# Weights of a hybrid decoder layer handed over as contiguous tiles, gate columns as one array, trial layouts of the fifth FFN pair removed

## The chip, the cores and the metric

The kernel runs on one core of a Trainium2 chip; the other cores are idle. The metric is device time in microseconds (us) of one launch. TensorE (PE) multiplies, with the loads of its stationary operand shown apart as PEld; VectorE (DVE) and ScalarE (ACT) do the elementwise work; GpSimd (POOL) does a few small operations; SyncE (SP) issues nearly all DMAs, which sixteen DMA engines carry out between HBM (DRAM) and the on-chip buffer.

## The reference

One layer of a decoder over 512 tokens of width 2048, in float32. With `h = RMSNorm(x)`, one projection feeds two groups of heads; their outputs are joined and projected back, and a SwiGLU network follows:

```python
proj = h @ w_in                       # w_in: 2048 x 6160
qa, ka, va, ra, ga, qb, kb, vb = split(proj)   # widths 512 512 1024 1024 16 1024 1024 1024
gate_pre = ga @ gla_gate_w2 + gla_gate_b       # rank 16
log_g = log_sigmoid(gate_pre) / 16
out_a = gla_mixer(qa, ka, va, ra, log_g)       # 4 heads, chunked gated linear attention
out_b = dilated_mixer(norm(qb), norm(kb), vb)  # 8 heads, three dilated branches, T5 bias
x = x + concat(out_a, out_b) @ w_out           # 2048 x 2048
h2 = RMSNorm(x)
x = x + (silu(h2 @ w_gate) * (h2 @ w_up)) @ w_down   # 2048 x 5632 twice, 5632 x 2048
```

The 16 columns `ga` are columns 3072 to 3087 of `w_in`.

## The kernel before

**Products.** All large products are made in pairs of 512 output columns with the seven-product scheme of Strassen and Winograd: `P1` to `P7` over quarters a, b, c, d of a weight pair, each in groups `g` of 512 rows of the contraction. A quarter is a tile of 128 partitions x 2 x 512 floats, 512 KB (`load_quarter`, L234): 256 rows and 512 columns of a weight matrix, of which two rows of 2 KB go to each partition. a and c come from the first block of 512 columns of the pair, b and d from the second. `Pair.source` (L265) gives the quarter, or a difference of two, made on VectorE in place (L271).

**Accuracy.** Each source is split into a high part (`first_part`, a cast on ScalarE, L374) and a low part (`second_part`, a subtraction on VectorE, L389). A group then has twelve products of 128 x 128 by 128 x 512 on TensorE: eight with the high part (two terms of the other operand, L190 and L191, built by `Operand`), four with the low part (L418). The moving operand is read through `folded` (L240), which interleaves the two halves of a row of 512.

**Order.** `stream` (L349) runs over all pairs in one hand-written order for TensorE, ScalarE and VectorE, one group ahead with the cast and two ahead with the source; background work (attention heads, transposes, building of operands) is dealt out between the groups by `step`. `first_pair` (L442) does the same for the first pair, with the operand's making interleaved by the table `FIRST`. Twelve buffers hold quarters (`wpool`); a load waits until the low part of the group that last used its buffer is made. The pairs are, in this order: six of the input projection, two of the output projection, eleven of the FFN (gate and up columns), six of the down projection.

**The start.** `LOADS` (L27) lists the first loads on SP: x in tiles of 256 KB, and a, b, c quarters of the first pair. `small_loads` (L644) follows at once: the remaining constants, then the 16 gate columns into `gaw` (L646), then small vectors (L647 to L650). `rank_weights` (L778, token `gprep`) regroups `gaw` on GpSimd (L782 to L784) and splits it with ScalarE (L793) and VectorE (L794). In `FIRST` it is followed by `g2`, a copy on VectorE (L625), and then by the transposes of further x tiles (L704).

**The trial layouts.** In the fifth FFN pair (`j == 4`) six of the 28 groups read the moving operand in other ways. `FORMS` names them by product and group. For four of the layouts (`LAYOUTS`) the parts are written rearranged, by two casts of 512 each (L369) and two subtractions (L382), and read through another pattern by `one_form` (L344); "split" reads the usual parts by two products of 256 columns (L337). The values computed are the same.

Of the kernel before, what the change touches and what calls it, by code (L numbers as in the profile page):

```python
# [10 lines left out]
F32 = mybir.dt.float32  # L11
# [7 lines left out]
P = 128  # L19
# [15 lines left out]

LAYOUTS = {
# [8 lines left out]
}  # L45
FORMS = {
    ("P1", 1): "four", ("P1", 2): "eight", ("P5", 1): "near", ("P5", 2): "line",
    ("P6", 1): "split", ("P6", 2): "four",
}
SINGLE = {"P1": "a", "P3": "d", "P2": "c"}  # L50
# [73 lines left out]
def block_kernel(ctx: ExitStack, tc: tile.TileContext, ins, out):  # L124
# [126 lines left out]
    class Pair:  # L251


        def __init__(self, op, rows, w1, w2, final, step, scale=None, before=None, forms=None):
            self.op, self.rows, self.w1, self.w2 = op, rows, w1, w2
            self.final, self.step, self.scale, self.before = final, step, scale, before
            self.q, self.dst, self.held, self.forms = {}, {}, {}, forms or {}

# [73 lines left out]

    def one_form(form, dst, left, right):

        if form == "split":
            for i in range(2):
                nc.tensor.matmul(  # L337
                    dst[:, 256 * i : 256 * i + 256], left,
                    halves(right)[:, :, 128 * i : 128 * i + 128].rearrange("p b a -> p a b"),
                    start=False, stop=False, skip_group_check=True,  # L340
                )
            return
        put, _, sizes, order = LAYOUTS[form]
        nc.tensor.matmul(  # L344
            dst, left, right.rearrange(order[0], **order[1]),
            start=False, stop=False, skip_group_check=True,
        )

    def stream(pairs):  # L349
# [9 lines left out]

        def form(k):  # L360
            p, prod, g = items[k]
            return p.forms.get((prod, g))

        def first_part(k):
            high[k] = hpool.tile([P, 2, 512], F32R, name=nm("wh"), tag="wh")
            if form(k) in LAYOUTS:
                put, get, sizes, _ = LAYOUTS[form(k)]
                for jj in range(2):
                    nc.scalar.copy(  # L369
                        high[k][:, jj].rearrange(put, **sizes),  # L370
                        sources[k][:, jj].rearrange(get, **sizes),
                    )
                return
            nc.scalar.copy(high[k], sources[k])  # L374

        def second_part(k):
            low[k] = hpool.tile([P, 2, 512], F32R, name=nm("wl"), tag="wl")
            if form(k) in LAYOUTS:
                put, get, sizes, _ = LAYOUTS[form(k)]
                src = sources.pop(k)  # L380
                for jj in range(2):
                    nc.vector.tensor_tensor(  # L382
                        low[k][:, jj].rearrange(put, **sizes),
                        src[:, jj].rearrange(get, **sizes),
                        high[k][:, jj].bitcast(F32).rearrange(put, **sizes),
                        op=ALU.subtract,
                    )
                return
# [8 lines left out]
        for k, (p, prod, g) in enumerate(items):  # L397
# [13 lines left out]
            for w, terms in ((high.pop(k), (0, 1)), (low.pop(k), (0,))):  # L411
                for jj in range(2):
                    for m in range(2):
                        for hl in terms:
                            if form(k):
                                one_form(form(k), p.dst[prod][m], a[:, jj, hl, m * P : (m + 1) * P], w[:, jj, :])
                                continue
                            nc.tensor.matmul(  # L418
                                p.dst[prod][m], a[:, jj, hl, m * P : (m + 1) * P], folded(w[:, jj, :]),
                                start=fresh and g == 0 and len(terms) == 2 and jj == 0 and hl == 0,  # L420
                                stop=g == p.op.groups - 1 and len(terms) == 1 and jj == 1,
                                skip_group_check=not fresh,
                            )
                if len(terms) == 2:
                    p.step()
# [218 lines left out]
    def small_loads():  # L644
        load(mats[:, 1:, :], ins["mats"][:, 1:, :])
        load(gaw, w_in[:, 3072:3088].rearrange("(k p) n -> p k n", p=P))  # L646
        load(gq, ins["q_norm_g"].rearrange("(p o) -> p o", o=1))  # L647
# [71 lines left out]

    col = lambda c: w_in[:, c : c + 512]  # L720
    opx = Operand(4)
# [560 lines left out]
    flow = rate((84, 0.5))  # L1282
    pair(opx, rows_in, col(3088), col(4112), final_proj("qb0", "kb0"), flow, row_scale)
    pair(opx, rows_in, col(5648), col(5136), final_proj("vb1", "vb0"), flow, row_scale)
    pair(opx, rows_in, col(3600), col(4624), final_proj("qb1", "kb1"), flow, row_scale)
    pair(opx, rows_in, col(2048), col(2560), final_gate, rate((27, 0.72), (1, 0)), row_scale)
# [81 lines left out]

    ocol = lambda c: w_out[:, c : c + 512]
    def output_scales():  # L1370
# [124 lines left out]
    for i in range(3):  # L1495
        g0 = 4 * i
        rows_d = [(512 * (g0 + g), 512 * (g0 + g) + 256) for g in range(opd[i].groups)]
        for np_ in range(2):
            c = 1024 * np_
            lead = np_ == 1 and i < 2  # L1500
            pair(
                opd[i], rows_d, w_down[:, c : c + 512], w_down[:, c + 512 : c + 1024],
                final_down(i, np_), paced([0] * 6) if lead else step,
                before=(lambda i=i: background.append(down_jobs(i + 1))) if lead else None,
            )
# [45 lines left out]
```

## Time and profile before

| | us |
|---|---|
| median of 3 runs | 1985.06 |
| the three runs | 1980.8 to 1986.24 |
| the profiled execution, first to last instruction | 1985.2 |
| mean granted clock of TensorE in it | 0.996 |

Times in the profile are in us from the first instruction. The granted clock is TensorE's share of full speed. A row of the chain of waits tells when a piece began, how long it lasted, and what it was; followed back from the end, each piece was released by the one before it. In a row of waits stand the waiting operation, what ended its wait, the total, the number of waits and the longest. "DMA tile<-tensor" is a transfer from its issue to its landing. The share of a DMA queue is the time of its packets as a share of sixteen engines' time in the window; packets overlap a little, so it can pass 100%.

### The profile page before, as it was taken

How to read it: one execution, taken by the hardware profiler on the slowest of the kernel's cores; microseconds unless marked ns; L12 is line 12 of the kernel's file. 1: busy time of each engine (PE TensorE's matmuls, PEld its weight loads, DVE VectorE, ACT ScalarE, POOL GpSimd, SP SyncE). 2: the span in 40 equal slices, each digit the busy share in tenths (PEclk: the TensorE clock that was granted, in tenths of full speed). 3: DMA queues.
4: the chain of work that ended last, by engine and by line, in shares of the span. 5: the costliest groups of instructions: out<-in, count | busy, mean ns of one | idle time of the engine just before them, and what ended most of it. 6: DMA issues, size and time to landing. Idle time of an engine off the chain costs nothing.

```text
span 1985.2 us, 25841 instructions
## 1 busy us (share of the span) xinstructions
PE 1936.2 (98%) x9238; PEld 1670.5 (84%) x9238; DVE 1655.3 (83%) x1855; ACT 1097.6 (55%) x1605; POOL 58.5 (3%) x81
## 2 busy tenths in 40 slices
PE   7999999999999889999999999999999999999998
PEld 6888888887878777888888888888888888888887
DVE  7997777768789789878878778778779989989987
ACT  6664564566666666545545545445446646546443
POOL 0000130011000001000000000000000000000000
PEclk9999999999999999999999999999999999999999
DMA  8357365454666685554553553554555855955762
GB/s 276 120 169 265 109 194 155 145 162 157 198 213 212 204 266 167 180 164 134 180 165 114 172 167 126 170 170 128 170 168 156 301 193 180 314 165 189 258 212 75
DMA packets 237113, 360.45 MB, mean 182 GB/s; under 512 B 18246, under 2 KB 96783, under 8 KB 236984
## 3 DMA queue, kind: packets, MB, share of 16 engines
q1 hardware_dynamic: 236776, 358.72, 56.9%
q8 instruction: 72, 1.18, 0.2%
q14 instruction: 57, 0.47, 0.1%
q10 hardware_dynamic: 208, 0.08, 0.0%
HBM read 296.59 MB, written 64.51 MB: 182 GB/s over the span
## 4 chain that ended last, share of the span: by engine, by line
PE 84%; DMA 7%; DVE 5%; issue 2%; ACT 1%; SPq 1%; POOL 0%; DVEq 0%; ACTq 0%; POOLq 0%
PE acc L418 74%; PE acc L486 3%; DVE wl L389 2%; PE bank L1129 1%; DVE wa L271 1%; PE acc L344 1%; PE bank L1036 1%; PE bank L1014 1%; DVE AS L191 1%; DMA xn_d<-oT 1%; DMA k<-in_w_in 0%; PE bank L1029 0%; DMA wc<-in_w_in 0%; DMA wb<-in_w_in 0%; PE bank L486 0%
## 5 line engine op out<-in xcount | busy, mean ns | idle before, releaser
L418 PE MATMUL acc<-wh,AS 128*128 128x512 f32 x2976 | 706.4, 380 | 1.5 <-DVE AS L191 1.0
L418 PEld LDWEIGHTS acc<-wh,AS 128*128 128x128 f32 x2976 | 561.5, 189 | 83.8 <-DVE AS L191 1.8
L374 ACT CAST wh<-wa 128x1024 fp32r<-128x1024 f32 x371 | 388.8, 1048 | 396.5 <-PE acc L418 354.4
L418 PE MATMUL acc<-wh,AA 128*128 128x512 f32 x2240 | 533.4, 381 | 5.8 <-ACT wh L374 5.7
L389 DVE TENSOR_TENSOR wl<-wa,wh 128x1024 fp32r<-128x1024 f32 x371 | 452.5, 1223 | 81.5 <-ACT wh L374 46.8
L418 PEld LDWEIGHTS acc<-wh,AA 128*128 128x128 f32 x2240 | 424.3, 190 | 68.4 <-ACT wh L374 8.0
L418 PE MATMUL acc<-wl,AS 128*128 128x512 f32 x1488 | 390.5, 385 | 8.7 <-DVE wl L389 8.6
L418 PEld LDWEIGHTS acc<-wl,AS 128*128 128x128 f32 x1488 | 276.5, 189 | 60.0 <-DVE wl L389 20.3
L418 PE MATMUL acc<-wl,AA 128*128 128x512 f32 x1120 | 294.5, 385 | 0.9 <-DVE wl L389 0.7
L418 PEld LDWEIGHTS acc<-wl,AA 128*128 128x128 f32 x1120 | 209.3, 190 | 32.4 <-DVE wl L389 3.1
L374 ACT CAST wh<-wb 128x1024 fp32r<-128x1024 f32 x94 | 98.5, 1049 | 117.3 <-PE acc L418 112.5
L374 ACT CAST wh<-wc 128x1024 fp32r<-128x1024 f32 x94 | 98.4, 1047 | 109.6 <-PE acc L418 99.9
L374 ACT CAST wh<-wd 128x1024 fp32r<-128x1024 f32 x94 | 98.6, 1049 | 105.1 <-PE acc L418 99.5
L271 DVE TENSOR_TENSOR wa<-wc,wa 128x1024 f32<-128x1024 f32 x94 | 114.9, 1227 | 45.2 <-DMA wc<-in_w_gate 25.3
L389 DVE TENSOR_TENSOR wl<-wd,wh 128x1024 fp32r<-128x1024 f32 x94 | 114.9, 1224 | 40.2 <-ACT wh L374 29.2
L389 DVE TENSOR_TENSOR wl<-wc,wh 128x1024 fp32r<-128x1024 f32 x94 | 115.0, 1224 | 36.4 <-ACT wh L374 36.3
L389 DVE TENSOR_TENSOR wl<-wb,wh 128x1024 fp32r<-128x1024 f32 x94 | 114.0, 1222 | 4.7 <-ACT wh L374 4.7
L271 DVE TENSOR_TENSOR wb<-wd,wb 128x1024 f32<-128x1024 f32 x94 | 115.0, 1224 | 1.8 <-DMA wd<-in_w_in 1.3
L271 DVE TENSOR_TENSOR wa<-wb,wa 128x1024 f32<-128x1024 f32 x94 | 113.8, 1222 | 0.8
L271 DVE TENSOR_TENSOR wa<-wd,wa 128x1024 f32<-128x1024 f32 x94 | 113.6, 1224 | 0.2
L313 DVE SCALAR_TENSOR_TENSOR seed<-acc,rs,seed 128x512 f32<-128x512 f32 x96 | 70.8, 749 | 29.2 <-PE acc L418 29.2
L297 ACT ACTIVATE seed<-acc,rs 128x512 f32<-128x512 f32 x96 | 60.8, 683 | 3.1 <-PE acc L418 2.9
(300 smaller groups left out, 1429.2 us busy)
## 6 DMA issues: line engine op xcount, KB each, us to landing
wa<-in_w_gate SPq DMA_DIRECT2D x44, 512.0 KB, 4.2
wb<-in_w_up SPq DMA_DIRECT2D x44, 512.0 KB, 4.4
wd<-in_w_up SPq DMA_DIRECT2D x44, 512.0 KB, 4.5
wc<-in_w_gate SPq DMA_DIRECT2D x44, 512.0 KB, 3.7
wc<-in_w_in SPq DMA_DIRECT2D x28, 512.0 KB, 3.8
wa<-in_w_in SPq DMA_DIRECT2D x24, 512.0 KB, 4.8
wb<-in_w_in SPq DMA_DIRECT2D x24, 512.0 KB, 6.1
wd<-in_w_in SPq DMA_DIRECT2D x24, 512.0 KB, 6.7
```

The lines of the kernel that those rows point to most:

```text
L191: nc.vector.tensor_tensor(a[:, :, 1, :], src, a[:, :, 0, :].bitcast(F32), op=ALU.subtract)
L271: nc.vector.tensor_tensor(src, self.quarter(one, g), src, op=ALU.subtract)
L297: nc.scalar.activation(halves(t), unfolded(src[m]), AF.Copy, scale=self.scale(half, m))
L313: nc.vector.scalar_tensor_tensor(halves(seed[m]), unfolded(src[m]), self.scale(half, m), halves(seed[m]), op0=ALU.mult, op1=ALU.add,)
L344: nc.tensor.matmul(dst, left, right.rearrange(order[0], **order[1]), start=False, stop=False, skip_group_check=True,)
L374: nc.scalar.copy(high[k], sources[k])
L389: nc.vector.tensor_tensor(low[k], sources.pop(k), high[k].bitcast(F32), op=ALU.subtract)
L418: nc.tensor.matmul(p.dst[prod][m], a[:, jj, hl, m * P : (m + 1) * P], folded(w[:, jj, :]), start=fresh and g == 0 and len(terms) == 2 and ...
L486: recent["pe"] = nc.tensor.matmul(dst[prod][m], a[:, jj, hl, m * P : (m + 1) * P], folded(w[:, jj, :]), start=fresh and g == 0 and len(ter ...
L1014: nc.tensor.matmul(lp[:, :n], qh[:, b * P : (b + 1) * P], kh[:, :n], start=True, stop=True)
L1036: nc.tensor.matmul(op, vh[:, k, :], lgs[b][:, k * P : (k + 1) * P], start=(k == 0), stop=(k == b))
L1129: nc.tensor.transpose(bk[:, jj, m * P : (m + 1) * P], tiles[m][:, f : f + P], ident)
```

## The change

The host hands `w_in`, `w_out`, `w_gate`, `w_up` and `w_down` over in another order: cut into quarters, each stored in one piece as it will lie on the chip, 4 KB for each partition. The 16 gate columns are taken out of `w_in` and handed over as an array of their own, 1 KB for each partition; the column numbers behind them fall by 16. The trial layouts with their branches are removed, so that the fifth FFN pair runs as the others do. Sizes, loads, products and their order stay.

```diff
 def load_quarter(rows, name, g, w):
     r0 = rows[g][0 if name in "ab" else 1]
     t = wpool.tile([P, 2, 512], F32, name=nm("w" + name), tag="w")
-    load(t, w[r0 : r0 + 256, :].rearrange("(j p) n -> p j n", p=P))
+    load(t, w[r0 // 256])
...
-    load(gaw, w_in[:, 3072:3088].rearrange("(k p) n -> p k n", p=P))
+    load(gaw, ins["gw"])
...
-    col = lambda c: w_in[:, c : c + 512]
+    col = lambda c: w_in[:, c // 512]
...
-LAYOUTS = {
...
-FORMS = {
...
-            if form(k) in LAYOUTS:
...
-                            if form(k):
-                                one_form(form(k), p.dst[prod][m], a[:, jj, hl, m * P : (m + 1) * P], w[:, jj, :])
-                                continue
...
-        c = slice(512 * j, 512 * j + 512)
         pair(
-            opn, rows_n, w_gate[:, c], w_up[:, c], final_ffn(j),
-            paced(paces.get(j, ())), tok_scale, forms=FORMS if j == 4 else {}, before=lambda j=j: before_ffn(j),
+            opn, rows_n, w_gate[:, j], w_up[:, j], final_ffn(j),
+            paced(paces.get(j, ())), tok_scale, before=lambda j=j: before_ffn(j),
         )
...
+    def blocks(w):
+        k, n = w.shape
+        return w.reshape(k // 256, 2, P, n // 512, 512).transpose(0, 3, 2, 1, 4)
+
     for name in _INS:
         a = np.asarray(inputs[name])
-        give(name, a if name == "rel_bias" else a[0])
+        a = a if name == "rel_bias" else a[0]
+        if name == "w_in":
+            give("gw", a[:, 3072:3088].reshape(16, P, 16).transpose(1, 0, 2))
+            a = np.delete(a, np.s_[3072:3088], axis=1)
+        if name in ("w_in", "w_out", "w_gate", "w_up", "w_down"):
+            a = blocks(a)
+        give(name, a)
```

The columns of `w_out` and `w_down` are chosen in the same way (`w_out[:, c // 512]`, `w_down[:, 2 * np_]`, `w_down[:, 2 * np_ + 1]`).

More of the change, by code (lines that the diff above doesn't have):

```diff
@@ L251, in block_kernel, with __init__ @@
     class Pair:
-        def __init__(self, op, rows, w1, w2, final, step, scale=None, before=None, forms=None):
+        def __init__(self, op, rows, w1, w2, final, step, scale=None, before=None):
             self.op, self.rows, self.w1, self.w2 = op, rows, w1, w2
             self.final, self.step, self.scale, self.before = final, step, scale, before
-            self.q, self.dst, self.held, self.forms = {}, {}, {}, forms or {}
+            self.q, self.dst, self.held = {}, {}, {}
         def quarter(self, name, g):
@@ L331, in end @@
                 self.close(self.held[which], src, *CLOSES[prod])
[L333 to L347, printed above, removed]
     def stream(pairs):
@@ L358, in total @@
             sources[k] = p.source(prod, g)
-        def form(k):
-            p, prod, g = items[k]
-            return p.forms.get((prod, g))
         def first_part(k):
             high[k] = hpool.tile([P, 2, 512], F32R, name=nm("wh"), tag="wh")
-            if form(k) in LAYOUTS:
[L367 to L373, printed above, removed]
             nc.scalar.copy(high[k], sources[k])
@@ L377, in second_part @@
             low[k] = hpool.tile([P, 2, 512], F32R, name=nm("wl"), tag="wl")
[L378 to L388, printed above, removed]
             nc.vector.tensor_tensor(
@@ L1282, in block_kernel @@
     flow = rate((84, 0.5))
-    pair(opx, rows_in, col(3088), col(4112), final_proj("qb0", "kb0"), flow, row_scale)
-    pair(opx, rows_in, col(5648), col(5136), final_proj("vb1", "vb0"), flow, row_scale)
-    pair(opx, rows_in, col(3600), col(4624), final_proj("qb1", "kb1"), flow, row_scale)
+    pair(opx, rows_in, col(3072), col(4096), final_proj("qb0", "kb0"), flow, row_scale)
+    pair(opx, rows_in, col(5632), col(5120), final_proj("vb1", "vb0"), flow, row_scale)
+    pair(opx, rows_in, col(3584), col(4608), final_proj("qb1", "kb1"), flow, row_scale)
     pair(opx, rows_in, col(2048), col(2560), final_gate, rate((27, 0.72), (1, 0)), row_scale)
@@ L1367, in first_columns @@
                 yield
-    ocol = lambda c: w_out[:, c : c + 512]
+    ocol = lambda c: w_out[:, c // 512]
     def output_scales():
```

7 lines of the change are left out of this document (1 added, 6 removed), and 8 rows, old and new, of the table LAYOUTS.

## The prediction

> **What bounds the kernel now.** I read the page's head first, then the granted clock, then the stretches of single FFN pairs, then the chain of waits where a stretch is longer than its neighbours.
>
> ```profile
> span 1985.2 us, 25841 instructions
> PE 1936.2 (98%) x9238; PEld 1670.5 (84%) x9238; DVE 1655.3 (83%) x1855; ACT 1097.6 (55%) x1605; POOL 58.5 (3%) x81
> ```
>
> TensorE is busy for 98% of the span, so a change pays only where TensorE itself stands still or is slowed. Stretches of one FFN pair (columns: PE, PEld, DVE, ACT, POOL busy, clock, DMA share, GB/s):
>
> ```profile
> 970.45:1044.77 74.32, 74.32 (x353) 65.01 (x353) 60.21 (x58) 37.16 (x43) 0.00 (x0) 1.00 0.51 159
> 1044.77:1124.01 79.24, 79.24 (x365) 65.88 (x365) 62.03 (x63) 39.65 (x48) 0.00 (x0) 1.00 0.49 150
> 1124.01:1198.31 74.30, 74.30 (x354) 65.02 (x353) 60.20 (x58) 37.14 (x43) 0.00 (x0) 1.00 0.51 156
> ```
>
> The fourth, fifth and sixth FFN pair run gapless at full clock with the DMA engines half idle: there weights are never late, and a faster load is worth nothing. One wait of VectorE on gate weights is long in total and costs TensorE nothing, because VectorE has 14 us to spare in each 74.3:
>
> ```profile
> DVE wa L271 <- DMA wc<-in_w_gate: 25.3, 34, 1.7
> ```
>
> What is left is the fifth pair, 4.9 us longer than its neighbours, and the start, where the only long stop of the first 100 us lies (chain of waits; start, length):
>
> ```profile
> 25.37 9.00 DMA k<-in_w_in
> ...
> 34.50 0.29 POOL v L782
> ...
> 35.56 0.36 ACT gs L793
> ...
> 36.22 0.18 DVE g L625
> ...
> 36.44 1.12 PE bank L704 x4
> ```
> ```profile
> 31.25:36.44 5.19, 0.00 (x0) 0.00 (x1) 0.80 (x3) 1.23 (x3) 1.47 (x5) 0.84 0.59 94
> ```
>
> The 128 KB of gate columns take 9.0 us to land, at 34.37. The weight preparation on GpSimd, the casts on ScalarE (L793) and VectorE (L794) and the copy L625 stand in line behind them; TensorE is empty for 5.19 us and restarts 2.07 us after the landing. Nothing else was late: the next cast of a weight (L466) follows L793 at once. SP was held as well, in the issue of the load behind this one (timeline of ScalarE, then of SP):
>
> ```profile
> 35.06 0.85 ACT L793 CAST gs<-v 128x192 fp32r<-128x192 f32 x2 [6.25 <-POOL v L783]
> 35.82 1.04 ACT L466 CAST wh<-wc 128x1024 fp32r<-128x1024 f32 x1
> ```
> ```profile
> 26.62 6.68 SPq L647 DMA_DIRECT2D gq<-in_q_norm_g  x1
> ```
>
> **The change part by part.** *The trial layouts.* All twelve products of a group run in 5.18/24 = 0.216 us each in the plain form (chain of waits in the fifth pair):
>
> ```profile
> 1050.81 7.32 PE acc L344 x20
> ...
> 1059.01 1.94 PE acc L344 x4
> 1060.95 5.18 PE acc L418 x24
> 1066.13 5.18 PE acc L344 x24
> ...
> 1076.49 2.68 PE acc L337 x24
> 1079.17 3.39 PE acc L344 x12
> ```
>
> Against 0.216 apiece (0.108 for the half-width L337) the groups lose 7.32 - 4.32 = 3.00, 1.94 - 0.86 = 1.08, 0, 2.68 - 2.59 = 0.09 and 3.39 - 2.59 = 0.80: 4.97 us. The stretches say the same: 79.24 - 74.31 = 4.93. I take **4.9**. The removed work on the other engines (62.03 - 60.2 us of VectorE, 39.65 - 37.15 of ScalarE) lies under TensorE and counts nothing; if VectorE were the bound it would be 1.8. The pair then is the same code as its neighbours, so neither bound is far: 4.5 to 5.0.
>
> *The gate columns as one array.* Before, 2048 rows of 64 B; after, 128 rows of 1 KB, each partition's 16 x 16 floats in one piece. What such rows cost the sixteen DMA engines, from three windows (24 to 30 us, then 10 to 22, then 31.6 to 33):
>
> ```profile
> DMA packets 1257, 2.43 MB, mean 405 GB/s; under 512 B 72, under 2 KB 72, under 8 KB 1257
> ...
> q1 hardware_dynamic: 1257, 2.43, 105.2%
> ```
> ```profile
> DMA packets 3490, 4.41 MB, mean 368 GB/s; under 512 B 204, under 2 KB 2467, under 8 KB 3490
> ...
> q1 hardware_dynamic: 3490, 4.41, 105.1%
> ```
> ```profile
> DMA packets 1722, 0.21 MB, mean 149 GB/s; under 512 B 1660, under 2 KB 1705, under 8 KB 1722
> ...
> q1 hardware_dynamic: 1722, 0.21, 100.7%
> ```
>
> The first window holds 2 KB packets almost alone: 1.052 x 16 x 6 us = 101 us over 1185 packets is 85 ns each. In the second, 202 us less 1023 of these leave about 115 us for 2263 packets of 1 KB: 50 ns. In the third, 22.6 us less some 4 for the 62 larger ones leave 11 ns for each of 1660 small packets. The gate columns thus need 2048 x 11 / 16 = 1.4 us of every engine, and 128 x 50 / 16 = 0.4 after: 1.0 saved as the least. The queue was already drained of weights in the third window, yet the landing came at 34.37; a slowest engine trails by over a microsecond, and with a quarter of the work I give that tail back by half a microsecond. **1.5** (1.0 to 2.4). SP is then free earlier for the small loads and the wd loads; TensorE waits for none of them now (from 36.44 its chain is products), so this is 0. The column numbers above 3088 move down by 16, which issues nothing.
>
> *Weights as tiles.* Each 512 KB load becomes 128 rows of 4 KB instead of 256 of 2 KB. No window shows 4 KB packets. Carrying on from 50 ns and 85 ns by the same 35 ns per KB gives an estimate of 155 ns; at an unchanged rate it is 2 x 85 = 170. The twelve weight loads ahead of the gate columns are 1536 such packets, 96 per engine: 96 x 15 ns = 1.4 us sooner at best, 0 at worst if the rate stays, below 0 if tiles read slower (a rival). The engines are full there, so it reaches the path. I take the middle, **0.7**. The stop at the start then ends 2.2 us sooner: 3.0 us remain of 5.19.
>
> The Trainium skill, page "DMA: Bandwidth & Descriptors", section Specifications, puts full line rate at transfers of 512 B and over, by which 2 KB rows have nothing to gain. The 1 KB and 2 KB rows above disagree mildly (2 x 50 is more than 85); by the page the time is the second rival's.
>
> *The clock.* After a stop TensorE runs at half clock for a while (waits of TensorE in three windows around 477, 741 and 663, then the stretches that follow and the start's):
>
> ```profile
> PE bank L1005 <- DMA q<-qb: 2.2, 1, 2.2
> ```
> ```profile
> PE acc L418 <- ACT wh L374: 2.6, 1, 2.6
> ```
> ```profile
> PE bank L1129 <- ACT qT L1315: 5.4, 1, 5.4
> ```
> ```profile
> 34.83:41.66 6.83, 5.22 (x15) 4.32 (x16) 5.57 (x9) 5.30 (x11) 1.15 (x4) 0.50 0.79 214
> ...
> 476.79:480.20 3.41, 3.37 (x25) 2.87 (x25) 3.41 (x6) 2.72 (x5) 0.00 (x0) 1.00 0.56 175
> 662.88:666.29 3.41, 3.32 (x9) 2.78 (x10) 0.41 (x2) 1.71 (x3) 0.00 (x0) 0.50 0.52 187
> 741.39:744.80 3.41, 3.07 (x7) 2.52 (x8) 3.14 (x5) 3.22 (x7) 0.00 (x0) 0.50 0.89 208
> ```
>
> A stop of 2.2 us left the clock alone, one of 2.6 halved it for 3.41 us, that of the start for 6.83. At half clock 5.22 us of work cost 2.6 too much at the start, and 3.07 cost 1.5 after 741. A stop of 3.0 us is nearest to that of 2.6, so I expect 1.5 in place of 2.6: **1.1** gained (0 to 2.6).
>
> The Trainium skill, page "TensorE: Matmul & The Clock Gate", Part 1, halves the clock only after at least one idle window of about 3.4 us. The 2.6 us row contradicts it as a bare threshold; by the page a 3.0 us stop leaves the clock up, which is the first rival.
>
> *Loads behind weights, later.* Two of the stops just shown end with small transfers that share the engines with weights (chain of waits before 663; waits of ScalarE):
>
> ```profile
> 647.16 5.79 DMA q<-in_x
> ...
> 653.76 4.77 DMA x_d<-q
> ...
> 658.60 3.51 DMA T<-x_d
> ```
> ```profile
> ACT AA L190 <- DMA top<-xn_d: 5.9, 2, 3.0
> ```
>
> With the 2.2 us stop these are five transfers on the path. If two weight loads stand ahead of each, 32 x 85 ns become 16 x 155 ns, 0.24 sooner: 1.2 in all. At worst each waits out one longer packet, 70 ns, 0.35 lost; at best all three stops (10.2 us) go. I take **1.0**, near the working by packet sizes: a trip of 3.5 to 5.8 us is mostly not weights ahead of it.
>
> Sum: 4.9 + 1.5 + 0.7 + 1.1 + 1.0 = 9.2 us, from the profiled 1985.2 to **1976.0**. The profiled span stands 0.1 above the median 1985.06 of three runs, which lie between 1980.8 and 1986.24, so the sum is carried over as it is.
>
> **The rivals.** *First: the clock stays up at the start*, because the stop shrinks under 2.3 us or because the window falls well. For it: 2.2 us was harmless. Against: 2.6 was not. The remaining 1.5 goes too: 1974.5.
>
> *Second: a byte in a 4 KB row costs as much as in a 2 KB row.* Only the gate columns and the trial pay: 0.7 and 1.0 fall out, 1977.7. For it: 405 GB/s in the 2 KB window against 368 where half are 1 KB, a small step already. Tiles that are still moved in 2 KB pieces, so that the change would not do what it says, give the same time.
>
> *Third: the start's stop is handed on.* If weights c and b, or the issue of the later loads, are the next to be late, the landing of the gate columns moves without TensorE: trial alone, 1980.3. For it: the engines are over 100% loaded up to that point. Against: at 35.82 ScalarE found its weight tile present.
>
> *Fourth, the other side: tiles read slower.* All partitions' rows now lie side by side, and if neighbouring engines then meet in the same part of HBM, each 4 KB packet takes D longer than 170 ns. The 96 packets at the start and five trips behind 16 packets each make 176 D. Packets do stretch in this kernel (window 840 to 1040):
>
> ```profile
> DMA packets 19514, 32.24 MB, mean 161 GB/s; under 512 B 1245, under 2 KB 6433, under 8 KB 19502
> ...
> q1 hardware_dynamic: 19502, 32.08, 52.6%
> ```
>
> 1683 us less 11 and 5188 x 50 ns leave 108 ns for each of 13069 packets of 2 KB, 28% over 85, at half the load. The same on tiles is D = 47 ns, 8.3 us: 1985.2 - 4.9 - 1.5 + 8.3 = 1987.1. It turns to a loss from D = 36 ns. Against: stretched packets now come with strided rows, so there is no sign that contiguous ones would be worse.
>
> **How the numbers follow.** Forecast 0.42, clock 0.20, no gain by size 0.17, handed on 0.13, slower tiles 0.08. The low end takes the trial, the whole stop and its slow clock (5.2 + 2.6) and 3 later: 1969. The high end is the trial alone with D of 10 ns on top: 1980.3 + 1.8 = 1982. What can be told from no change is 0.3%, 6.0 us, so faster means under 1979.1: nearly all of the forecast and of the clock case, most of the case without gain by size and a quarter of the handed-on stop, 0.78. Slower needs over 1991: half of the slower tiles, with a little for what I have not thought of, 0.05. The rest, 0.17, is neither.
>
> **What would show it.** The fifth pair at 74.3 us, without L344. The gate load landing in about 7 us instead of 9.0 and TensorE empty for some 3 us near 31. Packets of 2 KB and over falling by about 50 thousand (205 MB of weights by 4 KB). The half-clock stretch at the start 3.4 us long or gone. I am wrong if the stop at the start keeps its 5 us, if FFN pairs differ from 74.3, or if the weights' share of DMA time rises.

## The result and the profile after

The changed kernel takes 1977.08 us (median of 7 runs, 1974.87 to 1980.36) against 1985.06 (median of 7, 1980.8 to 1988.33) for the kernel before on the same chip: a ratio of 0.9959 with a 95% interval of 0.9948 to 0.9971, or 8 us less (6 to 10). The forecast was 1976.0. The profiled execution spans 1975.2 us, 10.0 less than the one before.

The head of the page after, its DMA line and the line of SP's DMA queue, and then the same two DMA lines from the page before:

```profile
span 1975.2 us, 25806 instructions
...
PE 1930.5 (98%) x9226; PEld 1669.3 (85%) x9226; DVE 1653.7 (84%) x1850; ACT 1096.0 (55%) x1600; POOL 55.0 (3%) x81
...
DMA packets 184505, 360.45 MB, mean 182 GB/s; under 512 B 16198, under 2 KB 94863, under 8 KB 184376
...
q1 hardware_dynamic: 184168, 358.72, 52.8%
```
```profile
DMA packets 237113, 360.45 MB, mean 182 GB/s; under 512 B 18246, under 2 KB 96783, under 8 KB 236984
...
q1 hardware_dynamic: 236776, 358.72, 56.9%
```

The same bytes travel in 52,608 packets fewer: 2048 of the gate columns have become 128, and the rest are weights whose two rows of 2 KB have become one of 4 KB. TensorE has twelve products fewer (the split layout made 24 of 12) and is busy 98% of the span as before.

The fifth FFN pair and the pairs around it (stretches; columns as in the prediction):

```profile
964.56:1038.86 74.30, 74.30 (x353) 65.00 (x353) 60.28 (x58) 37.12 (x43) 0.00 (x0) 1.00 0.46 159
1038.86:1113.16 74.30, 74.30 (x354) 65.00 (x353) 60.29 (x58) 37.11 (x43) 0.00 (x0) 1.00 0.45 160
1113.16:1187.46 74.30, 74.30 (x354) 65.01 (x353) 60.19 (x58) 37.12 (x43) 0.00 (x0) 1.00 0.46 156
```

79.24 us have become 74.30, like the neighbours: 4.94 us. The start (chain of waits, then three stretches) looks otherwise than forecast:

```profile
23.47 10.14 DMA k<-in_gw
...
33.74 0.23 POOL v L726
...
34.80 0.36 ACT gs L737
...
35.46 0.18 DVE g L569
...
35.68 1.11 PE bank L648 x4
```
```profile
26.00:31.57 5.57, 5.57 (x28) 4.40 (x26) 4.62 (x6) 2.63 (x6) 0.00 (x0) 1.00 1.01 391
31.57:35.68 4.11, 0.01 (x1) 0.00 (x0) 0.80 (x3) 1.23 (x3) 1.47 (x5) 0.82 0.84 249
34.17:41.00 6.83, 5.32 (x15) 4.41 (x16) 5.67 (x9) 5.30 (x11) 1.04 (x4) 0.50 0.62 232
```

The gate columns are asked for 1.9 us earlier (23.47 against 25.37) and land only 0.76 earlier (33.61 against 34.37): the transfer, with a sixteenth of the rows, lasts 10.14 us instead of 9.00. TensorE stands for 4.11 us instead of 5.19, and the half clock behind it is as long as it was, 6.83 us.

Where the 10 us of the two profiles went shows best at points of the program that both have. The table, worked out from the traces of all kernels of this study, takes the n-th cast of a weight on ScalarE; the first row is the start in the execution before, the others are differences to it:

```
                  first   gate    output   5th FFN  5th     first   last     span
                  pair    pair    proj.    pair     FFN     down    down
                  ends    starts  ends     starts   ends    pair    group
before            102.2   458.0   742.1   1043.9   1123.2  1571.6  1973.9  1985.2
after              -0.8    -2.5    -5.9     -5.9    -10.8   -12.7   -10.2   -10.0
e7_after_again     -1.3    -2.1    -5.6     -3.9     -8.9   -10.8    -8.6    -8.2
e1_trial_only      -1.3    -2.7    -2.7     -2.7     -7.7    -9.6    -7.4    -7.5
e2_gate_only       -2.1    -3.2    -7.2     -6.0     -6.0    -7.0    -4.4    -4.1
e3_tiles_only      -2.2    -4.1    -5.1     -5.1     -5.2    -5.7    -4.3    -4.4
e6_no_tiles        -0.9    -2.1    -0.7      1.5     -3.5    -5.1    -1.8    -1.9
e8_dense_2kb       -0.1    -0.3    -2.6      0.3     -4.7    -5.0    -4.1    -3.5
e4_gate_earlier    -3.3    -4.8    -6.8     -5.8    -10.8   -12.7   -13.0   -12.8
e5_scale_later     -7.4    -7.2   -10.0     -9.6    -14.5   -15.7   -15.9   -15.3
e12_best_again     -7.7    -8.4   -11.7     -9.4    -14.3   -15.9   -14.0   -13.3
e9_early_64b       -6.1    -4.2    -6.9     -5.3    -10.2   -11.6    -8.8    -8.6
e10_moves_only     -5.8    -5.1    -5.2     -3.0     -3.0    -4.1     0.7     1.0
e11_moves_again    -3.8    -2.4    -5.3     -2.6     -2.5    -3.7    -2.5    -2.1
```

It has to be read with the spread of single executions in mind. Two executions of one kernel differ by up to 2 us (after and e7, e5 and e12) or 3.2 us (e10 and e11). Between the first down pair and the last group, where of the edits only the tiles act, the rows move by -0.3 to +4.8 us, and by 1.2 to 4.8 in the five others with strided weights: the execution before was quick there. Only the fifth pair repeats to a tenth.

### The profile page after: what moved, and what is told of

It is laid out like the page before. It is cut to its first block, busy times and chain, and to the rows that moved or that the text cites. A ratio compares the mean times of both kernels' runs of the same rounds, so it can differ in the third digit from the quotient of the medians.

```text
span 1975.2 us, 25806 instructions
## 1 busy us (share of the span) xinstructions
PE 1930.5 (98%) x9226; PEld 1669.3 (85%) x9226; DVE 1653.7 (84%) x1850; ACT 1096.0 (55%) x1600; POOL 55.0 (3%) x81
## 3 DMA queue, kind: packets, MB, share of 16 engines
q1 hardware_dynamic: 184168, 358.72, 52.8%
## 4 chain that ended last, share of the span: by engine, by line
PE 79%; DVE 8%; DMA 8%; issue 3%; ACT 1%; SPq 1%; POOL 0%; DVEq 0%; ACTq 0%; POOLq 0%
PE acc L362 70%; DVE wl L336 3%; PE acc L430 3%; DVE wa L257 2%; PE bank L1073 1%; PE bank L980 1%; DMA k<-y_d 1%; PE bank L958 1%; DVE AS L177 1%; DMA T<-p_d 1%; DMA xn_d<-oT 1%; DMA k<-in_gw 1%; DVE seed L1251 1%; PE bank L973 0%; PE bank L430 0%
## 5 line engine op out<-in xcount | busy, mean ns | idle before, releaser
L362 PEld LDWEIGHTS acc<-wh,AS 128*128 128x128 f32 x3008 | 567.7, 189 | 84.0 <-DVE AS L177 1.8
L332 ACT CAST wh<-wa 128x1024 fp32r<-128x1024 f32 x376 | 394.0, 1048 | 400.3 <-PE acc L362 364.9
```

Source lines behind the costliest of these rows:

```text
L362: nc.tensor.matmul(p.dst[prod][m], a[:, jj, hl, m * P : (m + 1) * P], folded(w[:, jj, :]), start=fresh and g == 0 and len(terms) == 2 and ...
```

## The experiments

Each kernel was timed in five rounds beside the kernel before; all ratios are to it, with 95% intervals, and a ratio's thousandth is 2.0 us. In the edits, lines that only adapt column numbers or the host's arrays are left out; other lines left out are marked by three dots.

**The parts alone.** e1 is the kernel before without the trial layouts:

```diff
-            paced(paces.get(j, ())), tok_scale, forms=FORMS if j == 4 else {}, before=lambda j=j: before_ffn(j),
+            paced(paces.get(j, ())), tok_scale, before=lambda j=j: before_ffn(j),
```

> The kernel before without the trial layouts, nothing else changed. If their cost is what TensorE loses in the fifth pair, that pair takes 74.3 us instead of 79.2, the start is as before (gate columns landing near 34.4, a stop of 5 us), and the kernel is 4.9 us faster (ratio 0.9975). If the pair's time is handed on to a later wait, the pair shortens but the time moves by less than 2 us.

Measured: ratio 0.9968 (0.9956 to 0.9979), 6.4 us less, 4.2 to 8.7. By the table the pair itself gives 5.0 of it; the 4.9 of the prediction lies in the interval. What is beyond lies within the interval too: the profiled execution was 2.7 us ahead before the fifth pair, in stages that the edit does not touch.

e2 is the kernel before with the gate columns as an array; the weights stay strided and the layouts stay.

```diff
-        load(gaw, w_in[:, 3072:3088].rearrange("(k p) n -> p k n", p=P))
+        load(gaw, ins["gw"])
```

> The kernel before with the gate columns as one array, weights strided, trial layouts kept. Theory (a slowest DMA engine sets the landing, so that the smaller load gives little): landing 0.3 to 1.0 us sooner than before, the half-clock stretch still 6.8 us, the kernel 0 to 1 us faster. Rival (the prediction's step: the load's own work sets it): landing 1.5 us sooner, near 32.9, the kernel 1.5 to 2.6 us faster.

Measured: 0.9996 (0.9986 to 1.0006), 0.8 us less with 2 either way. By itself the array gains nothing that these runs can tell. The gate columns landed 1.2 us sooner in its profile, between what the two readings had put; the table further down shows how little one landing says.

e3 is the kernel before with the weights as tiles; the gate columns keep their rows of 64 B, read from a second, whole copy of `w_in`.

```diff
-    load(t, w[r0 : r0 + 256, :].rearrange("(j p) n -> p j n", p=P))
+    load(t, w[r0 // 256])
...
-        load(gaw, w_in[:, 3072:3088].rearrange("(k p) n -> p k n", p=P))
+        load(gaw, ins["w_in_rows"][:, 3072:3088].rearrange("(k p) n -> p k n", p=P))
```

> The kernel before with weights as tiles alone: gate columns still in 64 B rows (from a second, whole copy of w_in), trial layouts kept. Theory (the tiles shorten the later waits for loads between 200 and 800 us as well as the start): 3 to 5 us faster, with TensorE's stops in 400 to 800 us some 4 us shorter in sum and the landing of the gate columns 0.7 us sooner. Rival (what the profile of after shows beyond the trial and the start is the spread between executions): 0 to 2 us faster.

Measured: 0.9977 (0.9966 to 0.9988), 4.6 us less, 2.4 to 6.8. This rules out the slower tiles of the fourth rival and is more than the 1.7 us that the forecast gave the weights as tiles (0.7 at the start and 1.0 later). The 4 us less of stops between 400 and 800 us that went with the expectation were not seen: TensorE stands idle there for 23.6 us against 24.6.

**The array and the layouts without the tiles; the changed kernel again.** e6 is made from the kernel before and has the other two parts, so that it does what the changed kernel does, but with strided weights:

```diff
-        load(gaw, w_in[:, 3072:3088].rearrange("(k p) n -> p k n", p=P))
+        load(gaw, ins["gw"])
...
-            paced(paces.get(j, ())), tok_scale, forms=FORMS if j == 4 else {}, before=lambda j=j: before_ffn(j),
+            paced(paces.get(j, ())), tok_scale, before=lambda j=j: before_ffn(j),
```

> The kernel after with the weights strided again: trial layouts removed and gate columns as one array. If tiles are worth what they gave alone (4.6 us), it is 3 to 5 us slower than after, ratio to before near 0.998. If tiles and the gate array pay for the same wait at the start and add little else, it is 0 to 2 us slower than after, ratio near 0.9965.

> The kernel after, unchanged, as the second profile and on the same chip as the three beside it. Ratio to before 0.995 to 0.996. If the landing of the gate columns (33.6 us) is set by a lagging engine it lies between 33.0 and 34.0 again; the half-clock stretches may fall elsewhere.

Measured beside each other: e6 0.9979 (0.9970 to 0.9989), e7 0.9955 (0.9942 to 0.9968). The difference, 0.0024, is what tiles are worth when the other two parts are in: 4.8 us, with 3.2 either way if the two intervals are taken as independent. e6 gains 4.2 us (2.2 to 6.0), less than the forecast's 4.9 for the layouts and 1.5 for the array together. In e7 the gate columns landed at 34.1, outside the 33.0 to 34.0 that went with a lagging engine. Alone, the three parts gave 6.4, 0.8 and 4.6, 11.8 us in all, against 8.0 and 8.9 for the whole change; with some 2 us either way on each, that is no proof of an overlap.

Waits of TensorE between 500 and 820 us, after and then e6, suggest a single place (these two rows hold the stops of the output projection and of the attention ahead of it):

```profile
PE bank L1073 <- ACT qT L1259: 7.2, 3, 4.8
PE acc L362 <- ACT wh L332: 3.5, 2, 2.5
```
```profile
PE bank L1129 <- ACT qT L1315: 9.3, 3, 6.9
PE acc L418 <- ACT wh L374: 4.0, 3, 1.9
```

The first row holds the stop of 5.4 us near 660 that the prediction named, where small transfers run beside weights: 7.2 us in all with tiles, 9.3 without. But e2, strided too, has 7.4. As a mean the first row is 7.7 us in the seven profiles with tiles and 7.7 in the six with strided weights, the second 3.1 and 3.2, and the 2.2 us stop near 477 us became 1.9 and 2.0. So none of these stops carries the gain. From the table, the stretch from the gate pair's start to the end of the output projection is 2.7 us shorter than in the execution before as a mean of the seven profiles with tiles (after, e3, e4, e5, e7, e9, e12: 1.0 to 3.5) and 0.9 shorter as a mean of the six that have strided weights (before itself, e1, e2, e6, e10, e11: 4.0 shorter to 1.4 longer). That is 1.7 of the 4 to 5 us, less than the spread of the strided ones. Another 0.9 lies in the down projection (1.5 us longer than in the execution before with tiles, 2.4 with strided weights, as means), where TensorE waits 2.1 us for casts of weights with tiles and 3.8 without. The remainder is spread over the other stages in amounts smaller than their spread.

**Size or density?** e8 keeps each quarter in one piece but stores its two rows apart, so that a partition gets two packets of 2 KB:

```diff
-    load(t, w[r0 // 256])
+    load(t, w[r0 // 256].rearrange("j p n -> p j n"))
...
-        return w.reshape(k // 256, 2, P, n // 512, 512).transpose(0, 3, 2, 1, 4)
+        return w.reshape(k // 256, 2, P, n // 512, 512).transpose(0, 3, 1, 2, 4)
```

> The kernel after with each quarter still in one piece in HBM, but stored so that each partition gets two rows of 2 KB instead of one of 4 KB. If the tiles pay by the packet size, packets stay at 84 ns per 2 KB and the time is that of the kernel without tiles. If they pay because the bytes lie together, the time is that of after, and the mean 2 KB packet in the FFN falls well below 108 ns.

Measured: 0.9965 (0.9952 to 0.9978), between e7 and e6 and not to be told from either. By the time it stays open whether the tiles pay by the size of the packet or by lying dense. The packets speak against density: from 24 to 30 us, with the engines full, a dense row of 2 KB took 84.5 ns and the engines moved 403 GB/s (before: 84.7 and 405), and from 840 to 1040 us a dense row took 101 ns, as in e1 and e2 with strided rows (101), not well below 108.

**What decides the landing at the start.** The start of GpSimd's first copy, which follows the landing of the gate columns by 0.13 us, TensorE's stop and the end of it, and the half clock around that end (begin, length), from the profiles of the kernels that keep the load in its old place:

```
                 gate columns  weights     copy starts  TensorE stands  restarts  half clock
before           64 B rows     strided     34.50        5.19            36.44     34.83  6.83
e1_trial_only    64 B rows     strided     34.19        4.99            36.13     36.07  3.41
e2_gate_only     array         strided     33.33        4.00            35.27     35.47  3.41
e6_no_tiles      array         strided     34.54        4.55            36.48     36.68  3.41
e3_tiles_only    64 B rows     tiles       33.39        3.75            35.33     35.06  3.41
e8_dense_2kb     array         dense 2 KB  34.35        4.34            36.30     34.74  6.83
after            array         tiles       33.74        4.11            35.68     34.17  6.83
e7_after_again   array         tiles       34.23        4.47            36.17     35.95  3.41
```

Neither part moves the landing by more than executions of one form differ among themselves (33.33 and 34.54 for the array with strided weights). So the load's own rows were not what it took 9 us for. e4 tries the other reading, that it waits for what was asked for ahead of it: the changed kernel with this load issued before the last ten instead of behind them.

```diff
-    "u7 u5 a3 l7 c0 l2 l6 b1 c1 b0 c2 c3 b3 b2"
+    "u7 u5 a3 gw l7 c0 l2 l6 b1 c1 b0 c2 c3 b3 b2"
...
-        load(gaw, ins["gw"])
...
+        if what == "gw":
+            load(gaw, ins["gw"])
+            continue
```

> The kernel after with one load moved: the gate columns are issued ahead of the last ten loads of the list instead of behind them. If the landing of the gate columns is all that stops TensorE at the start, the stop shrinks from 4.1 us to under 1.5, the clock stays up, and the kernel is 4 to 7 us faster than after (near 1971). If the stop is handed on, to the last weights or to the issue of the later loads, it stays at 3 us or more and the time within 1 us of after.

Measured: 0.9951 (0.9936 to 0.9965); the interval overlaps that of the changed kernel (0.9948 to 0.9971). Timeline of SP, then of GpSimd, then the longest wait of TensorE in the first 100 us, all of e4:

```profile
13.16 0.34 SPq L669 DMA_DIRECT2D k<-in_gw  x1
```
```profile
19.60 4.52 POOL L728 COPY v<-k 128x128 f32<-128x128 f32 x1 [18.45 <-DMA k<-in_gw]
24.06 0.29 POOL L729 COPY v<-k 128x128 f32<-128x128 f32 x1
...
33.33 10.77 POOL L592 TENSOR_SCALAR gq<-gq 128x1 f32<-128x1 f32 x1 [8.47 <-DMA gk<-in_k_norm_g]
44.15 0.21 POOL L736 MEMSET gs<- 128x128 f32 x1
```
```profile
PE bank L757 <- POOL gs L736: 2.5, 1, 2.5
```

Asked for at 13.16, the columns are there at 19.5 (6.3 us later, instead of 10.1), fourteen microseconds sooner, and the 4 us stop is gone. In its place stands a stop of 2.5 us at 42: the scaling of `gq`, a product over 128 numbers, lasts 10.77 us, and the memset behind it on GpSimd holds TensorE. What ran beside it (stretch of e4):

```profile
33.33:44.10 10.77, 8.58 (x48) 7.57 (x47) 10.67 (x12) 10.74 (x26) 10.77 (x1) 1.00 0.56 203
```

VectorE is busy for 10.67 of the 10.77 us, and ScalarE for 10.74; the last section tells the two apart. In the changed kernel the same work of GpSimd falls into TensorE's stop, where VectorE is busy 0.80 of 4.11 us. e5 takes the scaling off GpSimd and puts it into the gate step, where VectorE does it in 0.14 us at 95.3 us; the result is first used at 346 us:

```diff
     def small_loads():
...
-        nc.gpsimd.tensor_scalar(gq, gq, 1.0 / math.sqrt(128.0), None, op0=ALU.mult)
...
     def gates():
...
+        nc.vector.tensor_scalar(gq, gq, 1.0 / math.sqrt(128.0), None, op0=ALU.mult)
```

> The fourth kernel (gate columns issued earlier) with the scaling of the query gains taken off GpSimd, where it held a memset back, and done by VectorE in the gate step. Theory (in the fourth kernel the stop was handed on to GpSimd, whose 0.3 us scaling took 10.8 us beside a busy VectorE): the 2.5 us stop near 44 us and its half-clock stretch go, the kernel is 3 to 4 us faster than the fourth, ratio to before near 0.993. Rival (the stop goes on to a next load or cast): TensorE still stops 2 us or more before 60 us and the ratio stays at 0.995.

> The fifth kernel once more, for a second profile and interval. If its lead over after holds, ratio to before 0.993 to 0.995, first pair done 6 to 8 us sooner than in before. If its first result was luck, ratio 0.9955 or above.

Measured: 0.9936 (0.9923 to 0.9948), and again on another chip 0.9936 (0.9924 to 0.9948): 12.7 us less than before. The changed kernel had 0.9959 and 0.9955; against their mean this is 0.0021 less, 4 us, with some 2.5 either way if the four intervals are independent. GpSimd's memset and TensorE's longest DMA wait of the first 100 us in e5, then the first 100 us of before, after and e12:

```profile
28.57 0.21 POOL L735 MEMSET gs<- 128x128 f32 x1 [3.39 <-PE bank L568]
```
```profile
PE bank L646 <- DMA x<-in_x: 1.2, 1, 1.2
```
```profile
10.00:105.00 95.00, 89.10 (x447) 77.79 (x446) 85.99 (x112) 67.56 (x123) 2.61 (x7) 0.96 0.60 201
```
```profile
10.00:105.00 95.00, 89.84 (x451) 78.62 (x450) 87.12 (x112) 68.10 (x123) 2.61 (x7) 0.96 0.56 207
```
```profile
10.00:105.00 95.00, 93.58 (x480) 82.20 (x479) 93.58 (x120) 71.14 (x127) 6.41 (x6) 1.00 0.61 223
```

In e12 TensorE is idle for 1.4 of these 95 us instead of 5.2 after, and the granted clock is 1.00 instead of 0.96: the stop and its half clock are both gone, and the first pair ends 7.7 us sooner than before. A smaller stop has come up later: in all five profiles with the scaling moved (e5, e9 to e12) TensorE waits 1.6 to 2.3 us near 137 us for a transfer (`v<-in_onehot`) that SP there issues behind a load of weights, and in none of the nine others. So the moves, too, handed on a part of what they gained.

**Does the array matter once it is early?** e9 is e5 with the gate columns as 64 B rows again, from a whole copy of `w_in`:

```diff
-            load(gaw, ins["gw"])
+            load(gaw, ins["w_in_rows"][:, 3072:3088].rearrange("(k p) n -> p k n", p=P))
```

> The fifth kernel with the gate columns read in 64 B rows again (from a second, whole copy of w_in), at the same early place. If the place decides and the form of the load does not, TensorE has no stop over 1 us after 15 us and the time is that of the fifth kernel, ratio to before 0.993 to 0.9945. If the form matters where the queue is full, the 1.4 us of engine time push the weights behind it, and the start loses 1 us or more.

Measured: 0.9954 (0.9941 to 0.9967), 3.6 us behind e5 and e12, by intervals that overlap by less than 0.001. It came out as the second half of the expectation, by another way than the engine time that this named. SP's timeline in e9 and in e5, and TensorE's waits in e9:

```profile
13.53 0.37 SPq L668 DMA_DIRECT2D k<-in_w_in_rows  x1
14.20 5.09 SPq L579 DMA_DIRECT2D x<-in_x  x1
```
```profile
13.39 0.34 SPq L668 DMA_DIRECT2D k<-in_gw  x1
14.13 0.38 SPq L579 DMA_DIRECT2D x<-in_x  x1
```
```profile
PE bank L646 <- DMA x<-in_x: 3.0, 2, 1.6
```

Behind the 2048 small rows SP is held for 5.09 us in the issue of the next load, an x tile, and all that follow leave later; TensorE waits 3.0 us for x instead of 1.2. At the old place the same hold (6.68 us before) fell on small vectors that nobody waited for.

**The two moves on the kernel before.** e10 and e11 are one kernel: before, with its strided weights, 64 B rows and layouts, and only the early load and the moved scaling.

```diff
-    "u7 u5 a3 l7 c0 l2 l6 b1 c1 b0 c2 c3 b3 b2"
+    "u7 u5 a3 gw l7 c0 l2 l6 b1 c1 b0 c2 c3 b3 b2"
...
-        load(gaw, w_in[:, 3072:3088].rearrange("(k p) n -> p k n", p=P))
...
-        nc.gpsimd.tensor_scalar(gq, gq, 1.0 / math.sqrt(128.0), None, op0=ALU.mult)
...
+        if what == "gw":
+            load(gaw, w_in[:, 3072:3088].rearrange("(k p) n -> p k n", p=P))
+            continue
...
+        nc.vector.tensor_scalar(gq, gq, 1.0 / math.sqrt(128.0), None, op0=ALU.mult)
```

> The kernel before with two moves alone: the gate columns (64 B rows) issued ahead of the last ten loads, and the scaling of the query gains taken off GpSimd. Weights strided, trial layouts kept. If the stop at the start was a matter of place, it goes here too: 5 to 7 us faster than before (ratio 0.9965 to 0.9975), about as much as the whole change brought. If tiles are needed for it, under 3 us.

> The tenth kernel (before with the two moves alone) once more, for a second profile. Its first profile was 5.8 us ahead of before at the end of the first pair and still 4 us ahead at the first down pair, and lost 5 us in the down projection. If that loss is the spread between executions, the down projection takes 402 to 405 us here and the ratio to before comes out at 0.997 to 0.998. If it belongs to the moves, the down projection takes 407 us again and the ratio stays above 0.9985.

Measured: 0.9994 (0.9984 to 1.0005) and 0.9986 (0.9978 to 0.9995), a gain of 1 to 3 us, though the table has the first pair ending 5.8 and 3.8 us sooner. The 5 to 7 us that the expectation gave to the place were missed, and by its words tiles would be needed. But e10 and e11 do not test that alone: they keep the rows of 64 B, and the hold that e9 showed behind such rows is here too (timeline of SP, then two waits of TensorE, e10):

```profile
13.89 5.15 SPq L635 DMA_DIRECT2D x<-in_x  x1
```
```profile
PE bank L660 <- DMA v<-in_onehot: 2.1, 1, 2.1
PE bank L702 <- DMA x<-in_x: 1.9, 1, 1.9
```

The two moves with the array and strided weights were not run, so whether tiles are needed stays open. Most of the lead is gone by the end, where e10 is 1.0 later and e11 2.1 sooner than before. Part of it goes in the down projection, where e10 takes 4.8 and e11 1.2 us longer than the quick execution before: in e10 TensorE waits 4.9 us there for casts of weights instead of 2.6, and 3.41 us of half clock follow the longest of these waits, where the execution before has no half clock. What takes the rest was not found.

## Why the prediction was right, and where it was not

**The total.** Time, sign and size were forecast: 9.2 us, of which 8.0 came by the medians and 10.0 by the profiles. The composition was not: one term was exact, three at the start mostly failed, one was too small, and the errors cancelled. That 9.2 came so near was luck beyond the 4.9 of the layouts.

**The trial layouts** (4.9): right, by the very row. The fifth pair became 74.30, and lost 4.9 to 5.0 us in each of the nine executions without the layouts in the table, and 0.1 at most in the others. The removed work of VectorE and ScalarE counted nothing, as put.

**The gate columns as one array** (1.5): wrong at this place. The step that failed took the 1.4 us of engine time of 2048 rows for a part of the 9.0 us to landing, and added half a microsecond for a slow engine's tail. The load without these rows took 10.14 us, and e2 gained 0.8 us with 2 either way. The 9 us were its place behind the other loads: e4, issued 10.3 us earlier and with ten loads fewer ahead of it, landed fourteen sooner. The third rival said that the stop would not care about the array, for another reason, that something else would be late at once; that is not what is seen, since the landing itself stayed. The prediction read SP's hold of 6.68 us and put it at nothing, rightly, as the x tiles were already asked for.

**Tiles at the start** (0.7) worked from an estimate of 155 ns for a packet of 4 KB. The stretch from 24 to 30 us after has such packets almost alone:

```profile
DMA packets 695, 2.48 MB, mean 414 GB/s; under 512 B 76, under 2 KB 97, under 8 KB 695
...
q1 hardware_dynamic: 695, 2.48, 101.7%
```

1.017 x 16 x 6 = 97.6 us, less 2 us for the 97 small ones, over 598 packets is 160 ns: the estimate was good and the second rival's 170 is too much. By the packets' own times a byte costs 6% less in rows of 4 KB than of 2 KB (160 ns against 2 x 85), but these times overlap, and what the full queue moved rose by 2% only (414 GB/s against 405). By the Trainium skill, page "DMA: Bandwidth & Descriptors", section Specifications, there would be no difference beyond 512 B; the measurement differs mildly, in the direction that the rows of before had shown. Yet the landing came 0.76 us sooner after and 0.27 in e7, with the array's share in it, and e6 and e3 show as much spread. So the time of a packet was right and the way to the path not shown: the load was asked for 1.9 us sooner and took 1.1 longer.

**The clock** (1.1): not delivered. It hung on the stop shrinking to 3.0 us; the stop is 4.11 and the half clock lasts 6.83 us as before. The first rival, that the clock stays up, fell for this change with the same premise. That the price follows the stop's length, which the term assumed, does not hold either: in the table of the eight starts the half clock lasts 6.83 us around stops of 5.19, 4.34 and 4.11 us, and 3.41 around five others of 3.75 to 4.99. In e7, the same kernel, a stop of 4.47 us has 3.41 us, half as much as that of 4.11. What decides it is told in the last section. Where the stop is really gone, as in e5 and e12, no half clock is seen at the start.

**Loads behind weights, later** (1.0): right in sign, too small, and not by the stops it named. Two contrasts give tiles 4.6 and 4.8 us in all, and little of it is at the start. The stage with the three stops is 1.7 us shorter with tiles as a mean of profiles, but the stops themselves differ by 0.1 us or less (2.0 against 1.9, 3.2 against 3.1, 7.7 and 7.7), so the five shorter trips behind weights are not what the runs show. Where the rest of the gain lies is not settled. Counting only stops with one releaser left out the short waits that are spread over the stages, but this is argued, not shown.

**The profile and the median.** The sum was set against the profiled span as if nothing lay around it. The profiled execution after took 1977.08 us as a run and spans 1975.2, so 1.9 us lie outside. Counted so, the execution before was one of about 1987, at the slow end of its runs; 9.2 less from the median instead would have been 1975.9, which changes nothing here.

**What would show it.** Of the signs given, the fifth pair, the fall of some 50 thousand packets and the smaller share of DMA time came; the landing in 7 us, the stop of 3 us and the shorter half clock did not. The stop kept 4.1 to 4.5 of its 5.2 us, between the two values that the prediction had told apart.

**The rivals.** Slower tiles: out, by e3 and by e7 against e6; the queue's share of DMA time fell from 56.9% to 52.8%. Rows of 4 KB do stretch where weights are never late: from 840 to 1040 us they took 185 to 215 ns in the seven profiles with tiles, against 160 at the start of after, much as strided rows of 2 KB took 101 to 108 against 85. No gain by size: e3 alone is 4.6 us faster, so out as put (it left the tiles nothing), though by its time e8 leaves open whether the packet's size is the reason. The stop handed on: not in the change, but it happened in e4, with another heir than the one named (GpSimd, not weights or issue).

## What to carry to other kernels

A load that lands late behind a full queue is late by its place: compare issue and landing with the load's own engine time (9 us against 1.4 here), and when the two are far apart, move it ahead instead of making it smaller. Before a stop is removed, list the work that it sheltered; what ran in its quiet (here GpSimd's small operations) can take many times as long beside a busy VectorE. And test the parts of a change one by one even when the total comes out as forecast: here the total was right with three of five terms wrong and a fourth too small, and the moves that the failed terms pointed to were worth another 4 us on the changed kernel, though only 1 to 3 on the kernel before, with its rows of 64 B.

## What the runs showed of the hardware

**GpSimd beside VectorE.** In the changed kernel, with VectorE nearly idle, the same two operations take 0.29 and 0.28 us (timeline of GpSimd, after):

```profile
33.74 0.29 POOL L726 COPY v<-k 128x128 f32<-128x128 f32 x1 [32.59 <-DMA k<-in_gw]
...
34.85 0.28 POOL L593 TENSOR_SCALAR gq<-gq 128x1 f32<-128x1 f32 x1
```

In e4 they took 4.52 and 10.77 us, with VectorE busy for all 4.52 us of the one and 10.67 of the other. The second copy of e4 (24.06) took 0.29 us with VectorE and ScalarE busy throughout, so busy engines alone do not do it. What VectorE ran before and beside it (timeline of VectorE, e4):

```profile
23.28 0.68 DVE L177 TENSOR_TENSOR AS<-xT,AS 128x512 fp32r<-128x512 f32 x1
23.89 0.68 DVE L654 TENSOR_TENSOR xT<-bank,g 128x512 f32<-128x512 f32 x1
```

From the start of the first copy to 23.89 every VectorE instruction reads two operands from the on-chip buffer; the one at 23.89 reads one of its two operands from `bank`, where TensorE puts its results, and the first copy ends 0.23 us behind its start. So it does in all six profiles with the early load (e4, e5, e9 to e12): the copy starts at 19.60 to 20.56, lasts 3.59 to 4.67 us, and ends 0.22 to 0.24 us behind the start of this instruction. The scaling of e4 stands likewise beside a gapless row of instructions with two such operands, and ends 0.1 us behind the last, at 44.0, when VectorE falls idle. The Trainium skill, page "GPSIMD Engine Reference", section Specifications, has the two engines share their interfaces to the on-chip buffer, with contention from VectorE instructions with two inputs in it; the rows agree. They show besides that GpSimd can be held through a whole row of such instructions, here for up to 10.5 us.

**The issue behind many small rows.** The DMA issued after 2048 rows of 64 B holds SP for 5.09 us (e9; 5.15 in e10 and 6.68 before), after the same bytes in 128 rows for 0.38 (e5). The load itself is issued in 0.37 and 0.34 us: the price is on the next one.

**The clock.** The same stop of 2.5 us near 735 us left the clock alone in one execution of the changed kernel and halved it in the other (timeline of TensorE, after and e7):

```profile
735.81 1.99 PE L362 MATMUL acc<-wh,AA 128*128 128x512 f32 x8 [2.48 <-ACT wh L332]
```
```profile
736.17 2.07 PE L362 MATMUL acc<-wh,AA 128*128 128x512 f32 x4 [2.51 <-ACT wh L332]
```

Eight products take 1.99 us in the one and four take 2.07 in the other. The fourteen profiles show on what it depends. Within an execution the clock falls to half and rises again only at points that lie whole steps of 3.413 us apart: before, it falls at 34.83, 662.88 and 741.39, which are 184 and 23 steps. What counts is how long TensorE is idle within one step. At full clock, up to 1960 us, all 37 steps with 2.0 us of idle time or more were followed by half clock; of 127 steps with 1.0 to 1.9 us four were (1.7 to 1.8 us, all near 470 us). At half clock the 41 steps with up to 0.5 us of idle time were followed by full clock, and the 12 with 0.7 or more by another half. Of the two stops above, the one that ended at 735.81 had 1.91 us in one step, and the one that ended at 736.17 had 2.03. At the start, TensorE restarted 1.5 to 1.6 us into a step of half clock in the three executions with 6.83 us, and before it or at most 0.3 us into it in the other five. So a stop of 2 to 5 us has no fixed price; it depends on where the stop falls on these steps.
